# Sums of the Strassen blocks written back into PSUM, and the last down steps done in two halves of the columns: a transformer block on one core of Trainium2

## The chip, the cores and the metric

The kernel runs on one core of a Trainium2 chip. It has five engines that matter here: PE (TensorE, the matrix multiplier, with PEld for its weight loads), DVE (VectorE), ACT (ScalarE), POOL (GpSimd) and SP (SyncE, which here only issues DMAs). SBUF is the core's working memory, PSUM the small memory into which PE adds up its products, in banks of 128 partitions by 512 fp32 numbers. The metric is the device time in microseconds (us) of one execution. For the kernel before, the median of three is 1511.14 us (1509.85 to 1515.28).

## What is computed

One layer of a hybrid encoder on x of 1024 positions and width 1024, in fp32, cut to what matters here:

```python
h = rms_norm(x, norm1)
proj = h @ w_in                                   # q, k, v of two mixers, forget logits, gates
qa, ka, va, fa, qc, kc, vc, gates = jnp.split(proj, SPLITS, axis=-1)
o_a = forgetting_attention(qa, ka, va, log_sigmoid(fa + forget_bias))   # 8 heads x 64, causal
o_b = chunk_band_attention(qc, kc, vc, rel_bias)                        # 8 heads x 64, a band
g_a, g_b = jnp.split(jax.nn.sigmoid(gates), 2, axis=-1)
merged = g_a * (o_a @ w_branch_a) + g_b * (o_b @ w_branch_b)
x = x + merged @ w_out
x = x + jnp.square(jax.nn.relu(rms_norm(x, norm2) @ w_up)) @ w_down     # width 4096 inside
return rms_norm(x, final_norm)
```

## The kernel before

Everything is held transposed: features on the 128 partitions, positions along the free axis in two halves of 512 (`hs(h)`). An fp32 matrix is split into a high and a low part (`fp32r`), and a product is three matmuls: high by high, high by low, low by high. `split` (L277) does that for an activation, ACT the high part and, mostly, DVE the low one; `split_w` (L163) does it for a weight, ACT (or POOL) the high part (L165), POOL the low one (L167).

The large products are done by a Strassen-like scheme, in units. A unit (`strassen_steps`, from L522) forms a block of 256 output features by 1024 positions as four tiles of 128 x 512, from seven products (`PRODS`), of four steps of three matmuls each, in four PSUM banks. While the products run, the tiles are put together: ACT copies the first product, p1 (L553); DVE forms u2 = bank 1 + p1 (L555), c22 = bank 2 + u2 (L557) and c22 = bank 3 + c22 (L559), which is output tile (1,1); bank 0 is tile (0,0) as it stands; and cc = bank + u2 (L567) makes the two others. c22 and cc go to SBUF tiles, and the function `out` of the stage reads them there, bank 0 in PSUM. Units take turns at two sets of four banks.

The order of the work, with the times at which it stands in the profiled execution:

- 0 to 320 us: load and norm of x, then 8 units of q and k (`project_qk`; `out` multiplies by the norm, L577) in turn with 4 units of v (`project_v`, L595), whose tiles are transposed on PE into banks of the second set (`vtp`, L604), split by ACT (`vs`, L278) and DVE (L279), and stored to DRAM.
- 320 to 430 us: the gate units (`project_gate`; `gate_out`, L391: multiply by the norm, then a sigmoid on ACT, L392, and a store of z, L393), interleaved with the row maxima of the first two heads (`s`, L499 on PE, L506 on DVE), whose transposed result goes out on ACT's queue as `m_rows` (L514). For unit 7, the last, `GPOOL` puts three of the four multiplications on POOL.
- 444 to 740 us: attention of 16 heads, with the branch products as fillers. 740 to 820 us: the other branch products and the merge. 820 to 906 us: the output projection; its last blocks give the operands of the up product (`late_operands`; the high part of T4 is an ACT cast), and unit 28, the first of 16 up units, starts with them. Norm 2 is worked out inside that unit: `norm2_stat` before the fourth finished product, `norm2` at the end (`rms`, `newton`, `spread`).
- 906 to 1190 us: the up units (`out`: relu and norm in one DVE instruction, L929, square on ACT, L930, store, and differences for the down product, L937).
- 1190 to 1499.6 us: the down product, the same scheme turned round: the seven products A11, S1, S2, S3, S4, A12, A22 over 16 steps k each, four tiles m a step, with the activations read back from DRAM.
- 1499.6 us to the end, 1515.9 us: the finish of the left half (h = 0). The last three steps of A22 (k = 13 to 15) run tile by tile: 9 matmuls of 128 x 512 for each of four tiles m. As a tile ends, `between` adds the bank to the accumulator (L1025), ACT squares (L234), DVE adds up the squares (L235), and ACT scales by the final gain (L998). `finish` then works out the norm of all 512 positions (`n_s` on PE, L266, Newton steps on DVE, L240 to L244, spread over the partitions by PE, `n_b`, L250), copies it to SBUF (L1007), multiplies the eight tiles (DVE L1016 six of them, POOL L1014 two) and stores each as 128 x 512 (L1017).

A scheduler places the instructions of each engine; `TO`, `VO`, `AO` and `LO` mark those that keep the written order. `tc.issue_after` holds an instruction behind another one in that order only.

## Time and profile before

| | |
|---|---|
| median of three runs | 1511.14 us (1509.85 to 1515.28) |
| the profiled execution's own time | 1517.57 us |
| its span in the trace | 1515.9 us |
| PE busy | 1458.9 us, 96% of the span |
| DVE busy | 958.2 us, 63% |
| POOL busy | 871.5 us, 57% |
| ACT busy | 730.4 us, 48% |
| mean share of the granted clock of PE | 0.983 |
| read and written in DRAM | 179.42 and 86.34 MB |

In a row of the timeline stand the start, the busy time, the engine, the line, the operation with its tiles (out<-in, numbers left out), and the count of instructions that run on from one another; in brackets the idle time ahead of the instruction and what ended it. Rows of groups give busy time in all and the mean of one instruction in ns. The windows give busy time of each engine in a stretch of the span, the granted clock of PE, the DMA engines' share and GB/s. In a row of a DMA queue stand its packets, MB, and its share of the time of 16 DMA engines.

### The profile page before, as it was taken

What the parts mean: (1) busy time and instruction counts of PE and PEld (TensorE: products, weight loads), DVE (VectorE), ACT (ScalarE), POOL (GpSimd) and SP (SyncE); (2) the same over time, 40 slices, a digit from 0 to 9 for tenths busy, and PEclk for the clock granted to TensorE, in tenths of its full rate; (3) what the DMA queues carried; (4) which work ended last, traced back from release to release, by engine and by line L of the source; (5) the groups of instructions that cost most, each with busy time, mean ns of one, the idle gap of its engine ahead of it and who ended that gap; (6) DMA issues with size and microseconds to landing.
All of it is one profiled execution on the core that took longest, in us unless ns stands there. A gap on an engine that the chain in (4) does not pass through costs nothing.

```text
span 1515.9 us, 20994 instructions
## 1 busy us (share of the span) xinstructions
PE 1458.9 (96%) x6774; PEld 1208.0 (80%) x6774; DVE 958.2 (63%) x1528; ACT 730.4 (48%) x1388; POOL 871.5 (57%) x712
## 2 busy tenths in 40 slices
PE   8999999999889889999999999999999999999996
PEld 5777888888668778888787888888888888888885
DVE  7755456644368678766424687666666557999543
ACT  8633333254348768657524553333333344444643
POOL 2478787778742223111076467888888555558462
PEclk9999999999989989999999999999999999999998
DMA  8546678763587698876466424444443776589363
GB/s 268 153 117 171 186 196 227 184 203 128 166 186 182 157 169 198 191 197 162 155 198 209 165 73 167 153 152 151 151 151 132 248 261 200 154 253 222 93 205 115
DMA packets 153039, 267.18 MB, mean 176 GB/s; under 512 B 22552, under 2 KB 40216, under 8 KB 149792
## 3 DMA queue, kind: packets, MB, share of 16 engines
q1 hardware_dynamic: 78544, 141.02, 30.6%
q10 hardware_dynamic: 50448, 84.27, 17.6%
q0 software_dynamic: 23936, 40.54, 12.6%
q8 instruction: 53, 0.87, 0.2%
q14 instruction: 58, 0.48, 0.1%
HBM read 179.42 MB, written 86.34 MB: 175 GB/s over the span
## 4 chain that ended last, share of the span: by engine, by line
PE 41%; POOL 4%; DMA 2%; DVE 2%; issue 2%; ACT 1%; SPq 0%; DVEq 0%; ACTq 0%; POOLq 0%
PE u L218 19%; PE dS L218 9%; PE dA L218 8%; PE o L218 4%; POOL wl_S L167 1%; PE dA L96 1%; POOL m L835 1%; POOL ml L279 1%; DMA olt<-o_dram 1%; DMA wr<-wall 0%; POOL accw L991 0%; DMA rb<-r_dram 0%; DMA z<-z_dram 0%; DVE T2l L279 0%; DVE B22l L279 0%
## 5 line engine op out<-in xcount | busy, mean ns | idle before, releaser
L167 POOL TENSOR_TENSOR wl_A<-wr,wh_A 128x512 fp32r<-128x512 f32 x118 | 165.8, 1412 | 81.1 <-ACT wh_A L165 63.8
L167 POOL TENSOR_TENSOR wl_S<-S,wh_S 128x512 fp32r<-128x512 f32 x102 | 139.4, 1371 | 30.2 <-ACT wh_S L165 29.9
L279 DVE TENSOR_TENSOR tl<-p,th 128x512 fp32r<-128x512 f32 (+1 forms) x192 | 109.6, 593 | 30.6 <-ACT th L278 26.3
L165 ACT CAST wh_A<-wr 128x512 fp32r<-128x512 f32 x105 | 65.0, 620 | 102.2 <-DMA a_dram<-at 53.0
L165 ACT CAST wh_S<-S 128x512 fp32r<-128x512 f32 x105 | 63.8, 618 | 86.7 <-POOL S L190 35.5
L278 ACT CAST th<-p 128x512 fp32r<-128x512 f32 (+1 forms) x192 | 92.6, 509 | 12.2 <-PE pv L752 5.7
L167 POOL TENSOR_TENSOR wl_S<-ks,wh_S 128x512 fp32r<-128x512 f32 x48 | 68.1, 1446 | 52.6 <-ACT wh_S L96 48.7
L506 DVE CUSTOM_DVE_ANT_0 s<-s,bc 128x384 f32<-128x384 f32 (+3 forms) x128 | 69.8, 564 | 36.6 <-PE s L499 22.9
L499 PE MATMUL s<-qk 128*128 128x384 f32 (+2 forms) x192 | 63.4, 362 | 20.9 <-DMA qk<-qk_dram 14.5
L567 DVE TENSOR_TENSOR cc<-u,u 128x512 f32<-128x512 f32 x70 | 48.0, 686 | 54.9 <-PE u L218 54.7
L188 POOL TENSOR_TENSOR S<-wr,wr 128x512 f32<-128x512 f32 x35 | 49.5, 1415 | 56.8 <-DMA wr<-wall 51.0
L930 ACT ACTIVATE v<-v 128x512 f32<-128x512 f32 x64 | 40.5, 632 | 62.3 <-DVE v L929 62.3
L751 PE MATMUL pv<-th,v 128*128 128x512 f32 (+1 forms) x192 | 66.9, 348 | 1.0 <-ACT on L764 0.9
L728 PE MATMUL st<-qk 128*128 128x512 f32 (+1 forms) x192 | 67.0, 352 | 0.1
L736 PE MATMUL st<-sk 82*128 82x512 f32 (+1 forms) x192 | 66.1, 346 | 0.0
L752 PE MATMUL pv<-th,v 128*64 128x512 f32 (+1 forms) x192 | 66.0, 344 | 0.0
L753 PE MATMUL pv<-tl,v 128*128 128x512 f32 (+1 forms) x192 | 66.0, 344 | 0.0
L167 POOL TENSOR_TENSOR wl_A<-ka,wh_A 128x512 fp32r<-128x512 f32 x32 | 46.1, 1449 | 33.8 <-ACT wh_A L96 33.8
L278 ACT CAST qkh<-qk 128x512 fp32r<-128x512 f32 x32 | 19.9, 621 | 91.7 <-DMA qk_dram<-qkl 34.6
L748 ACT ACTIVATE p<-st,ncq 128x512 f32<-128x512 f32 (+1 forms) x96 | 54.0, 597 | 16.2 <-PE st L744 11.3
L499 PEld LDWEIGHTS s<-qk 128*128 128x128 f32 x192 | 36.7, 201 | 29.7 <-DMA qk<-qk_dram 13.5
L218 PE MATMUL u<-B11h,wh_A 128*128 128x512 f32 x140 | 56.2, 402 | 3.4 <-DVE vs L279 3.4
(404 smaller groups left out, 4959.6 us busy)
## 6 DMA issues: line engine op xcount, KB each, us to landing
wr<-wall SPq DMA_DIRECT2D x243, 256.0 KB
qk<-qk_dram POOLq DMA_DIRECT2D x16, 1024.0 KB, 6.3
a_dram<-at ACTq DMA_DIRECT2D x64, 256.0 KB
xT<-a_dram SPq DMA_DIRECT2D x64, 256.0 KB
qk_dram<-qkh ACTq DMA_DIRECT2D x96, 128.0 KB
a_dram<-v ACTq DMA_DIRECT2D x48, 256.0 KB
xB<-a_dram SPq DMA_DIRECT2D x44, 256.0 KB
z_dram<-zt ACTq DMA_DIRECT2D x32, 256.0 KB
```

What stands on the lines that cost most here:

```text
L165: (act.tensor_copy if act is G else act.copy)(wh, src)
L167: eng.tensor_tensor(wl, src, wh.bitcast(F32), op=ALU.subtract)
L218: done = eng.matmul(bank, w[wi], x[xi], start=(first and t == 0), stop=(t == n - 1 and not part), skip_group_check=part or not first)
L278: A.copy(dst[0], src)
L279: eng.tensor_tensor(dst[1], src, dst[0].bitcast(F32), op=ALU.subtract)
L499: T.matmul(ps[:, :n], qk[:, 1, i * P:(i + 1) * P], qk[:, 0, ks:ks + n], start=True, stop=not diag)
L506: V.tensor_tensor_reduce(ps[:, :v], ps[:, :v], bc[:, b0:b0 + v], 1.0, prev, ALU.add, ALU.min, out)
L728: T.matmul(ps[:, c], qk[:, 0, keys], qk[:, 1, qs], start=True, stop=False)
L736: T.matmul(ps[:, c], sk[:, 0, keys], sk[:, 1, qs], start=False, stop=not extra)
L751: T.matmul(pv[:, c], v3[hh][:, j, 1:3, :], th[:, c], start=first, stop=False)
L752: T.matmul(pv[0:HD, c], v3[hh][:, j, 0, :], th[:, c], start=False, stop=False)
L753: T.matmul(pv[:, c], v3[hh][:, j, 1:3, :], tl[:, c], start=False, stop=last)
```

## The change

**Sums stay in PSUM.** In every unit of projections, gates and up product, c22's last sum is written over bank 1, and the two cc over the banks that they are read from; `out` reads them in PSUM. No multiplication, sum, cast or store is dropped.

**Gates.** `GPOOL` becomes empty: the three multiplications of unit 7 go from POOL to DVE.

**The first up unit.** For k = 3 the high part of T4 is a DVE copy and not an ACT cast. The Newton steps of norm 2 and of the final norm keep v and t in columns 8 and 16 of the PSUM tile of the statistics. Unit 29's weight preparation is held behind unit 28's third-last low part (`behind`); POOL's order of those instructions is what it was.

**The end.** The last three steps of A22 run over two halves of 256 positions, q = 0 and 1, each with its own sums, squares and scaling; a half's norm is worked out by itself. For q = 0 the norm's sum stands behind q = 1's second tile on PE, the eight multiplications are on POOL and read a copy of the norm in SBUF, and its four stores (two tiles each, 128 x 2 x 256) are on SP. For q = 1 the eight multiplications are on DVE and read the norm in PSUM; its eight stores of 128 x 256 alternate between SP and ACT.

```diff
-GPOOL = (7,)
+GPOOL = ()
...
-    def rms(name, ps):
-        r = cpool.tile([P, 2, 4], F32, tag="nr", name=f"{name}_r", bufs=2)
-        v, y = r[:, 0, :], r[:, 1, :]
+    def rms(name, ps, n=4):
+
+        y, v, t = cpool.tile([P, 2, 4], F32, tag="nr", name=f"{name}_r", bufs=2)[:, 0, 0:n], ps[:, 8:8 + n], ps[:, 16:16 + n]
...
             elif n == 3:
-                V.tensor_tensor(c22, banks[3], c22, op=ALU.add)
-                out(1, 1, c22)
+                V.tensor_tensor(banks[1], banks[3], c22, op=ALU.add)
+                out(1, 1, banks[1])
...
-                t = mk("cc")
-                V.tensor_tensor(t, banks[b], u2, op=ALU.add)
-                out(*((0, 1) if n == 5 else (1, 0)), t)
+                V.tensor_tensor(banks[b], banks[b], u2, op=ALU.add)
+                out(*((0, 1) if n == 5 else (1, 0)), banks[b])
...
-        split(xop["T4", k], t2, V)
+        if k == 3:
+            V.tensor_copy(xop["T4", k][0], t2)
+            V.tensor_tensor(xop["T4", k][1], t2, xop["T4", k][0].bitcast(F32), op=ALU.subtract)
+        else:
+            split(xop["T4", k], t2, V)
...
-    def finish(ps_pool, h, tiles, engs):
-
-        y = norm_stat(ps_pool, f"n3_{h}", accs[h])
+    def finish(ps_pool, h, tiles, engs, q=0, w=HALF):
+
+        cols = slice(q * w, (q + 1) * w)
+        eng = T if h else TO
+        y = norm_stat(ps_pool, f"n3_{h}{q}", accs[h][:, cols], eng)
...
-                dst = t[:, m, :]
+                dst = t[:, m, cols]
                 if engs[n % len(engs)] is G:
-                    G.tensor_tensor(dst, dst, rstd[:, hs(h)], op=ALU.mult)
+                    G.tensor_tensor(dst, dst, scale, op=ALU.mult)
                 else:
                     V.tensor_tensor(dst, dst, pb, op=ALU.mult)
-                (load, store)[n % 2](outT[:, m + 4 * row, hs(h)], dst)
+                out = outT[:, :, h * HALF + q * w:h * HALF + (q + 1) * w]
+                if engs != (G,):
+                    (load, store)[n % 2](out[:, m + 4 * row, :], dst)
+                elif m % 2:
+                    load(out[:, m + 4 * row - 1:m + 4 * row + 1, :], t[:, m - 1:m + 1, cols])
...
-            rest = between(n, banks)
-            for m in range(4):
-                for k in range(15 - STAG, 16):
-                    multiply(m, k)
-                next(rest)
+            rest, w = iter(()), HALF // 2
+            for q in range(2):
+                cols = slice(q * w, (q + 1) * w)
+                for m in range(4):
+                    for k in range(15 - STAG, 16):
+                        multiply(m, k, cols)
+                    V.tensor_tensor(au[:, m, cols], banks[m][:, cols], au[:, m, cols], op=ALU.add)
+                    final(au, m, 1, 0, cols)
+                    if m % 2:
+                        next(rest, None)
+                for _ in rest:
+                    pass
+                rest = finish(psm[1], 0, (p1, au), (V,) if q else (G,), q, w)
```

How the change moves instructions is seen at three places. The first is PE's queue at the seam of unit 9 (q and k) and unit 17 (v); `vtp` are the transposes of the v tiles of unit 16, `u17_0` is unit 17's first bank. Before:

```order
L218 MATMUL u9_3_941<-T4h_122,wl_9_A22_936 128x512
L604 MATMUL vtp_1085<-ident_66,vt_848 128x128 x4
L604 MATMUL vtp_1098<-ident_66,vt_862 128x128 x4
L218 MATMUL u17_0_1214<-B11h_170,wh_17_A11_1180 128x512
L218 MATMUL u17_0_1214<-B11l_174,wh_17_A11_1180 128x512
L218 MATMUL u17_0_1214<-B11h_170,wl_17_A11_1182 128x512
L604 MATMUL vtp_1111<-ident_66,vt_878 128x128 x4
```

And with the change:

```order
L220 MATMUL u9_3_937<-T4h_122,wl_9_A22_932 128x512
L610 MATMUL vtp_1079<-ident_66,vt_846 128x128 x4
L610 MATMUL vtp_1092<-ident_66,vt_860 128x128 x4
L220 MATMUL u17_0_1208<-B11h_170,wh_17_A11_1174 128x512
L220 MATMUL u17_0_1208<-B11l_174,wh_17_A11_1174 128x512
L220 MATMUL u17_0_1208<-B11h_170,wl_17_A11_1176 128x512
L220 MATMUL u17_0_1208<-B11h_170,wh_17_A11_1174 128x512
L220 MATMUL u17_0_1208<-B11l_174,wh_17_A11_1174 128x512
L220 MATMUL u17_0_1208<-B11h_170,wl_17_A11_1176 128x512
L610 MATMUL vtp_1105<-ident_66,vt_875 128x128 x4
```

The third transpose stands one group of three matmuls later, and so does the fourth, further on; the same in the three other units of v.

The second place is the seam of the gates and attention, on POOL, before (`wl_ab` are low parts of branch weights, `sk0` rows of the first head's operands):

```order
L167 TENSOR_TENSOR wl_ab2_0_7164<-wr21_0_7160,wh_ab2_0_7162 128x512
L391 TENSOR_TENSOR zt_4034<-c22_3750,rstd_96 128x512
L167 TENSOR_TENSOR wl_ab3_0_7435<-wr21_3_7431,wh_ab3_0_7433 128x512
L167 TENSOR_TENSOR wl_ab4_0_7608<-wr22_0_7604,wh_ab4_0_7606 128x512
L391 TENSOR_TENSOR zt_4108<-cc_4106,rstd_96 128x512
L391 TENSOR_TENSOR zt_4144<-cc_4142,rstd_96 128x512
L167 TENSOR_TENSOR wl_ab5_0_7862<-wr22_3_7858,wh_ab5_0_7860 128x512
L703 DMA sk0_4214<-m_rows_101 2x1024
```

With the change the last two of them stand on DVE, between the row maxima (`s`) of head 0:

```order
L573 TENSOR_TENSOR u7_2_3712<-u7_2_3712,u2_3715 128x512
L395 TENSOR_TENSOR zt_4071<-u7_2_3712,rstd_96 128x512
L510 ISA s_4017,st_4016<-s_4017,bc0_0_2889 128x384
L510 ISA st_4016 128x1
L573 TENSOR_TENSOR u7_3_3713<-u7_3_3713,u2_3715 128x512
L510 ISA s_4020,mn0_0_3897<-s_4020,bc0_0_2889,st_4016 128x256
L510 ISA mn0_0_3897 128x1
L395 TENSOR_TENSOR zt_4106<-u7_3_3713,rstd_96 128x512
```

The unit's last sums are the same instructions as before with another target; the three `zt` are new on this queue, the last of them behind head 0's last maximum (`mn0_0`), and POOL's low parts have nothing between them now.

The third place is the end of the program. PE before, from the last product of the last tile (`n3_0_s` the sums of squares, `n3_0_b` the spread norm):

```order
L96 MATMUL dA22_3_14911<-xT4h15_15206,wh_A22_15_15210 128x512
L96 MATMUL dA22_3_14911<-xT4l15_15207,wh_A22_15_15210 128x512
L96 MATMUL dA22_3_14911<-xT4h15_15206,wl_A22_15_15212 128x512
L266 MATMUL n3_0_s_15282<-ones_71,rstd_96 128x1 x4
L250 MATMUL n3_0_b_15296<-ident_66,n3_0_r_15287 128x128 x4
```

With the change, at the end of the second half's second tile (`n3_00` is the norm of the first half, `n3_01` that of the second):

```order
L96 MATMUL dA22_1_14836<-xT4l15_15134,wh_A22_15_15137 128x256
L96 MATMUL dA22_1_14836<-xT4h15_15133,wl_A22_15_15139 128x256
L96 MATMUL n3_00_s_15237<-ones_71,rstd_96 128x1 x2
L96 MATMUL dA22_2_14837<-xT4h13_15087,wh_A22_13_15093 128x256
L96 MATMUL dA22_2_14837<-xT4l13_15088,wh_A22_13_15093 128x256
```

And behind the last tile's products:

```order
L96 MATMUL dA22_3_14838<-xT4l15_15134,wh_A22_15_15137 128x256
L96 MATMUL dA22_3_14838<-xT4h15_15133,wl_A22_15_15139 128x256
L96 MATMUL n3_00_b_15276<-ident_66,n3_00_r_15240 128x128 x2
L96 MATMUL n3_01_s_15292<-ones_71,rstd_96 128x1 x2
L96 MATMUL n3_01_b_15303<-ident_66,n3_01_r_15295 128x128 x2
```

The first half's sum is in the stream of products now, its spread directly behind the last product. And on DVE, with the change, from the last tile's sum on:

```order
L1116 TENSOR_TENSOR accu_12289<-dA22_3_14838,accu_12289 128x256
L246 TENSOR_SCALAR n3_00_s_15237<-n3_00_s_15237 128x2
L237 TENSOR_TENSOR rstd_96<-rstd_96,sq_15258 128x256
L247 TENSOR_TENSOR n3_00_r_15240<-n3_00_r_15240,n3_00_s_15237 128x2
L237 TENSOR_TENSOR rstd_96<-rstd_96,sq_15272 128x256
L276 TENSOR_SCALAR n3_01_s_15292<-n3_01_s_15292 128x2
L243 RECIPROCAL n3_01_r_15295<-n3_01_r_15295 128x2
L244 TENSOR_TENSOR n3_01_s_15292<-n3_01_s_15292,n3_01_r_15295 128x2
L245 TENSOR_TENSOR n3_01_s_15292<-n3_01_s_15292,n3_01_r_15295 128x2
L246 TENSOR_SCALAR n3_01_s_15292<-n3_01_s_15292 128x2
L247 TENSOR_TENSOR n3_01_r_15295<-n3_01_r_15295,n3_01_s_15292 128x2
L1034 TENSOR_TENSOR accp1_12288<-accp1_12288,n3_01_b_15303 128x256 x4
```

The first half's last Newton steps stand behind the last tile's sum, two instructions apart, and the eight multiplications of the second half (four of them are the last row) follow its own Newton steps.

More of the change, by code (lines that the diff above doesn't have):

```diff
@@ L248, in spread @@
         pb = ps_pool.tile([P, HALF], F32, tag="d", name=f"{name}_b")
-        for c in range(4):
+        for c in range(y.shape[1]):
             eng.matmul(pb[:, c * P:(c + 1) * P], y[:, c:c + 1].to_broadcast([P, P]), ident, start=True, stop=True)
@@ L520, in strassen_unit, with strassen_steps @@
             pass
-    def strassen_steps(u, ps_pool, mk, out, start=(), between=None, before=None, cut=0):
-        ws = strassen_w(u, V if between else G, ALL[:cut] if cut else FIRST if between else ALL)
+    def strassen_steps(u, ps_pool, mk, out, start=(), between=None, before=None, cut=0, behind=()):
+        with ExitStack() as order:
+            for ins in behind:
+                order.enter_context(tc.issue_after(ins))
+            ws = strassen_w(u, V if between else G, ALL[:cut] if cut else FIRST if between else ALL)
         late, out_ = [], out
@@ L938, in out @@
                 store(a_dram[XI[n], u], t)
-        strassen_unit(U_UP + u, psm[u % 2], etile3, out, start=() if u else START2, before=None if u else (norm2_stat, norm2))
+        strassen_unit(U_UP + u, psm[u % 2], etile3, out, start=() if u else START2, before=None if u else (norm2_stat, norm2),
+                      behind=late)
+        late = () if u else (lows[-3].ins,)
     hstack.close()
@@ L1005, in finish @@
             yield
-        pb = spread(ps_pool, f"n3_{h}", y)
-        A.copy(rstd[:, hs(h)], pb)
+        pb = spread(ps_pool, f"n3_{h}{q}", y, eng)[:, 0:w]
+        scale = accs[h][:, cols]
+        if G in engs:
+            A.copy(scale, pb)
         yield
```

43 lines of the change are left out of this document (22 added, 21 removed).

## The prediction

> **What bounds the kernel now.** I read the engines' shares first, then the windows by stage, to see where PE stands still; then the waits and the timeline at those places, and the groups of instructions for the prices. The page's row of engines:
>
> ```profile
> PE 1458.9 (96%) x6774; PEld 1208.0 (80%) x6774; DVE 958.2 (63%) x1528; ACT 730.4 (48%) x1388; POOL 871.5 (57%) x712
> ```
>
> PE bounds the whole; DVE is busy 63% of the time. The windows give start and end, length, busy time of PE, PEld, DVE, ACT and POOL, the granted clock, the DMA share and GB/s:
>
> ```profile
> 120.00:136.00 16.00, 12.60 (x49) 10.01 (x48) 8.28 (x16) 6.91 (x16) 12.59 (x10) 0.89 0.77 224
> 400.00:444.00 44.00, 32.13 (x136) 25.02 (x134) 22.88 (x64) 11.25 (x20) 30.32 (x30) 0.87 1.01 246
> 444.00:740.00 296.00, 283.19 (x1585) 244.84 (x1585) 212.90 (x584) 218.84 (x478) 64.74 (x93) 0.96 0.72 170
> 906.00:1366.00 460.00, 460.00 (x2031) 380.50 (x2030) 324.12 (x335) 184.79 (x314) 323.31 (x239) 1.00 0.55 181
> 1499.60:1515.90 16.30, 3.06 (x16) 2.68 (x16) 6.06 (x15) 2.27 (x5) 2.49 (x2) 0.65 0.35 129
> ```
>
> In up and most of down (906 to 1366) PE is busy for 460.00 of 460.00 us at the full clock, so no other engine's work can be bought off there. PE stands still in four places: 3.4 us near 128, 11.9 us before attention, 12.8 us inside it, and 13.2 of the last 16.3 us. A change of DVE's work can pay only there.
>
> **The sums in PSUM.** Their prices, from the groups of instructions (busy us in all, mean ns of one):
>
> ```profile
> L929 DVE SCALAR_TENSOR_TENSOR v<-cc,rstd 128x512 f32<-128x512 f32 x32 | 51.8, 1619 | 0.5
> L929 DVE SCALAR_TENSOR_TENSOR v<-u,rstd 128x512 f32<-128x512 f32 x16 | 11.0, 690 | 18.2 <-PE u L218 17.8 <-ACT rstd L921 0.4
> L567 DVE TENSOR_TENSOR cc<-u,u 128x512 f32<-128x512 f32 x70 | 48.0, 686 | 54.9 <-PE u L218 54.7
> L506 DVE CUSTOM_DVE_ANT_0 s<-s,bc 128x512 f32<-128x512 f32 x40 | 28.2, 704 | 3.0 <-PE s L499 2.2 <-PE s L502 0.6
> ```
>
> The consumer that reads cc in SBUF takes 1619 ns, the one that reads bank 0 in PSUM 690: some 0.9 us less for each of 32 tiles, 29.7 us of DVE in the up stage alone, if the PSUM reader's price holds. The sum itself costs 686 ns; written over PSUM I take it at 704, the price of the row maxima that write over their own bank. All of it lies beside a PE that is busy for every microsecond of 906 to 1366, so it brings nothing there. The place where it could is a wait for DVE:
>
> ```profile
> 119.35 1.52 DVE L595 TENSOR_TENSOR vt<-c,rstd 128x512 f32<-128x512 f32 x1
> 127.30 0.65 ACT L278 CAST vs<-vtp 128x256 fp32r<-128x256 f32 x2 [4.01 <-DMA wr<-wall]
> 127.70 0.76 DVE L279 TENSOR_TENSOR vs<-vtp,vs 128x256 fp32r<-128x256 f32 x2 [2.57 <-ACT vs L278]
> 128.18 0.50 PE L218 MATMUL u<-B11h,wh_A 128*128 128x512 f32 x1 [3.40 <-DVE vs L279]
> PE u L218 <- DVE vs L279: 3.4, 1, 3.4
> PE u L218 <- DVE c L557: 0.7, 1, 0.7
> ```
>
> PE waits for DVE's split of a transpose bank, but DVE waited 2.57 us for ACT there, and ACT 4.01 us for a DMA. The faster vt at 119.35 is 7 us too early to matter. I take 0 for the sums. Below: the 0.7 us wait for c goes. Above: the moved transposes are three matmuls later in four units, 12 x 0.227 = 2.7 us (the pitch is in the next rows but one), if the banks that they free are waited for in each; before, PE waits for them in one unit only. What hides the 0 is slack of the bank sets, which alternate from unit to unit.
>
> **The gates.** Three multiplications go from POOL to DVE, and the z stores behind them are earlier in ACT's queue:
>
> ```profile
> L391 POOL TENSOR_TENSOR zt<-cc,rstd 128x512 f32<-128x512 f32 x2 | 2.5, 1274 | 0.4 <-DVE cc L567 0.4
> 438.13 0.33 ACTq L393 DMA_DIRECT2D z_dram<-zt  x1
> 438.83 2.18 PE L499 MATMUL s<-qk 128*128 128x256 f32 x7 [2.74 <-DMA qk<-qk_dram]
> 445.30 0.63 PE L736 MATMUL st<-sk 82*128 82x512 f32 x1
> ```
>
> On DVE two of them stand ahead of row maxima of head 0, 2 x 0.7 = 1.4 us; PE then waits 2.74 us for the second head's qk by DMA, which covers them; without this cover they cost 1.4. On ACT the stores of z now stand ahead of head 0's `m_rows`. I take 0. Below: one POOL multiplication, 1.3 us, off the way of the branch weights' low parts. Above: two z stores of 256 KB ahead of the qk load: 512 KB at the window's 246 GB/s is 2.1 us.
>
> **Attention** is reshuffled by the scheduler with the same instructions. Of 12.8 us of idle PE I allow a quarter, 3.2 us, either way, and take 0.
>
> **The first up unit.** Two rows of the timeline:
>
> ```profile
> 894.06 0.62 ACT L278 CAST T4h<-t 128x512 fp32r<-128x512 f32 x1 [5.19 <-DVE t L866]
> 895.73 0.50 PE L218 MATMUL u<-B21h,wh_A 128*128 128x512 f32 x1 [0.20 <-ACT p L553]
> ```
>
> Without the T4h cast ACT copies p 0.62 us earlier, and PE's wait of 0.20 us goes: -0.2. T4l isn't earlier, since DVE makes the copy itself, about as long. `behind` moves nothing in POOL's order: 0. The Newton scratch in PSUM changes no length that the end of the unit waits for by more than 0.1: 0.
>
> **The end.** The timeline from the last product on:
>
> ```profile
> 1499.17 0.39 PE L96 MATMUL dA<-xT4h,wl_A 128*128 128x512 f32 x1
> 1499.60 0.69 DVE L1025 TENSOR_TENSOR accu<-dA,accu 128x512 f32<-128x512 f32 x1
> 1500.32 0.63 ACT L234 ACTIVATE sq<-accu 128x512 f32<-128x512 f32 x1 [0.65 <-DVE accu L1025]
> 1501.73 1.05 PE L266 MATMUL n_s<-ones,rstd 128*128 128x1 f32 x8 [2.17 <-DVE rstd L235]
> 1502.82 0.16 DVE L272 TENSOR_SCALAR n_r<-n_s 128x4 f32<-128x4 f32 x1 [1.14 <-PE n_s L266]
> 1504.34 2.01 PE L250 MATMUL n_b<-ident,n_r 128*128 128x128 f32 x8 [1.56 <-DVE n_r L244]
> 1506.39 0.59 ACT L1007 COPY rstd<-n_b 128x512 f32<-128x512 f32 x1 [3.11 <-PE n_b L250]
> 1507.01 1.88 DVE L1016 TENSOR_TENSOR accp<-accp,n_b 128x512 f32<-128x512 f32 x3 [2.72 <-ACT rstd L1007]
> 1507.72 0.96 SPq L1017 DMA_DIRECT2D outT<-accp  x2
> ```
>
> Three phases follow on one another: norm (1499.6 to 1506.4), multiplications, stores. The half-width prices come from tiles of 256 columns elsewhere: two matmuls in attention, then DVE's and ACT's split of the v transposes, and POOL's low part of `near` (shortest, median, longest ns):
>
> ```profile
> 459.93 0.28 PE L751 MATMUL pv<-th,v 128*128 128x256 f32 x1
> 460.04 0.28 PE L752 MATMUL pv<-th,v 128*64 128x256 f32 x1
> 1498.94 0.39 PE L96 MATMUL dA<-xT4l,wh_A 128*128 128x512 f32 x1
> L278 ACT CAST vs<-vtp x32: 365/374/384, 120.8 to 253.2; 128x256 fp32r<-128x256 f32 x32
> L279 DVE TENSOR_TENSOR vs<-vtp,vs x32: 406/416/426, 121.2 to 253.6; 128x256 fp32r<-128x256 f32 x32
> L279 POOL TENSOR_TENSOR nbl<-near,nbh x8: 717/735/746, 332.7 to 530.5; 128x256 fp32r<-128x256 f32 x8
> ```
>
> And the stores, as the DMA view has them for 1506 to 1516 (40 slices of 0.25 us, then one of the two hardware queues), with the software queue of 510.5 to 515, whose packets are of 512 bytes:
>
> ```profile
> GB/s 0 0 0 0 0 0 0 0 0 0 287 369 344 402 385 393 360 385 393 393 377 377 377 360 402 369 369 385 385 385 401 393 99 0 0 0 0 0 0 0
> q1 hardware_dynamic: 576, 1.05, 28.6%
> q0 software_dynamic: 496, 0.25, 29.1%
> ```
>
> Data flows from 1508.5, 0.8 after the first store is issued, at about 375 GB/s until 1514.1; the span ends 1.8 later. Let T be 1499.6, when the last product is done; before, the span ends at T+16.3.
>
> PE: 72 matmuls at 0.118 (half the pitch of 1498.94 to 1499.17, and near the 0.11 of 459.93 to 460.04) for 36 at 0.227 are 8.50 for 8.17, +0.3; the first half's `n_s` in line, half of 1.05, +0.5: the last product is done at T+0.8. From there, in us:
> - the last sum 0.42, a Newton step 0.2, the third tile's squares 0.4, the last Newton step 0.2: the first norm at 1.2;
> - its spread on PE, half of 2.01, to 2.2; the copy (0.37) to 2.65; POOL from 2.7, a pair every 2 x 0.735: 4.2, 5.6, 7.1, 8.6;
> - the second half's `n_s` to 2.75, its Newton steps as before (1502.82 to 1504.34, 1.5) to 4.3, its spread to 5.3; DVE's eight multiplications at 0.42 from 5.4 to 8.8;
> - stores: the first pair's data from 5.0 (0.8 after its end), 0.26 MB, done by 5.9; the second pair's from 6.4, and from there both engines give more than the DMA takes, so 1.83 MB flow at its rate.
>
> That rate is the open price: a row of a store is 1 KB now and was 2 KB. A packet of 0.5 KB took 0.291 x 4.5 us x 16 / 496 = 42 ns of an engine, one of the tail (1.82 KB on average) 0.286 x 10 us x 16 / 576 = 79 ns. The line between them gives 56 ns for 1 KB, 16 x 1.024 KB / 56 ns = 290 GB/s. So 1.83 MB take 6.3 us, until 12.7; with 1.8 behind, T+0.8+14.5 = T+15.3, and the end gains 1.0. At 375 GB/s it would be 4.9 us, a gain of 2.4; at 195, the rate of the 0.5 KB packets (16 x 0.512 KB / 42 ns), 9.4 us, a loss of 2.1. I take 290, which the two rows give.
>
> The Trainium skill ("DMA: Bandwidth & Descriptors", Specifications) says that a transfer of 512 bytes or more runs at line rate; by it the rows of 1 KB would lose nothing, and the end would gain 2.4. The 42 ns of a 0.5 KB packet, which are half the time of one over three times its size, speak against it, though that queue is POOL's.
>
> **The sum**: -1.0 - 0.2 = -1.2. The profiled execution took 1517.57 us, 1.67 over its span; it would take 1516.4. It was 6.4 over the median of the runs, and the same difference from that, 1511.14 - 1.2, is 1509.9, the forecast.
>
> **Rivals.**
> *The stall at 128 goes (faster).* The PSUM sums shift DVE's and ACT's work in the v units, and the split comes before it is waited for. It would give the 3.40 us of idle and the lowered clock around it, 16 us x (1 - 0.89) = 1.8: 5.2 in all, 1504.7. For it: the chain's last link is DVE, which loses 0.8 us a tile in these units. Against it: DVE waited there itself, and the transposes now come later. 0.13.
> By the Trainium skill ("TensorE: Matmul & The Clock Gate", Part 1) the clock halves after an idle window of about 3.4 us that is free-running; the trace agrees in the size of this one wait, followed by a clock of 0.89 in that window.
> *Attention is entered later (slower).* The z stores ahead of the second head's qk load delay it by 2.1 us, and PE's 2.74 of waiting becomes 4.8. It decides from the point where it is longer than the 3.40 us after which the clock was lowered at 128: then another 1.8 is lost at that clock. -1.2 + 2.1 + 1.8 = +2.7: 1513.8. For it: the DMA share is 1.01 there. Against it: a matmul at 445.30 takes 0.63 instead of 0.39, so that the clock is lowered there already, and part of it can't be lost again. 0.15.
> *The stores of 1 KB run as fast as those of 2 KB.* The end gains 2.4: 1511.14 - 2.6 = 1508.5. For it: DVE and POOL give enough, and a hardware queue may do better than the software one. Against it: the line of packets above. 0.12.
> *The scheduler's new order in attention is worth more than 3.2 us*, in either direction: 1506 or 1514 at least. Nothing in the profile tells which. 0.06.
> The forecast keeps 0.54.
>
> **Range and chances.** The forecast's own range: the bounds of the parts, put together as independent ones: down 1.4 (end), 0.7, 1.3, 3.2, in all 3.8; up 3.1, 2.7, 2.1, 3.2, in all 5.6: 1506.1 to 1515.5. To hold 8 in 10 it reaches down through the first rival with half of that spread, to 1503.0, and up to 1515.5, which takes in the second rival. A measurement of this kernel can tell about 0.5%, 7.6 us, from no change: faster is below 1503.6, slower above 1518.7. Below lie two fifths of the first rival (0.05), half of the scheduler's case on that side and the forecast's tail: 0.12. Above, little of the second rival and the other tail: 0.04. The rest, 0.84, is the same.
>
> **What would show it.** Right: cc's consumers at about 0.7 us and DVE's busy time some 30 us lower in up alone, with PE's 906 to 1366 unchanged; the last product 0.8 later against the stage's start; the norm of the first half used on POOL while the second is worked out; stores at about 290 GB/s; a span after T of some 15.3. Wrong: the stall near 128 gone, or a new one with the transposes; more than 11.9 us of idle PE between 400 and 444; stores at 375 GB/s or at 195; or a wait of PE inside the last 72 matmuls for the first half's squares.

## The result and the profile after

The changed kernel takes 1506.1 us in the median of 12 runs (1499.28 to 1510.48), the kernel before 1512.39 in 12 (1506.77 to 1518.69). The ratio is 0.9947, with a 95% interval from 0.9931 to 0.9962: 8.0 us less by the ratio, between 5.7 and 10.4 (the two medians alone are 6.3 apart), where 1.2 less was forecast. The two profiled executions are 12.0 us apart (1517.57 and 1505.53), because that of before lies at the upper end of its runs; so a difference between these two traces counts here only where other traces show it too.

The row of engines of the changed kernel, and its window over up and most of down:

```profile
PE 1452.9 (97%) x6810; PEld 1205.7 (80%) x6810; DVE 890.9 (59%) x1548; ACT 733.1 (49%) x1396; POOL 841.6 (56%) x715
906.00:1366.00 460.00, 460.00 (x2031) 380.59 (x2029) 283.11 (x340) 186.32 (x315) 311.25 (x245) 1.00 0.57 180
```

DVE has 67 us less to do and up is still PE's alone. What was not expected is POOL: 29.9 us less, of which the three multiplications that left it explain 3.8. A part of that, 9.6 us, lies in one of its groups. First the low parts of weights as before had them, then with the change, then the consumer of up and the sum over the bank with the change:

```profile
L167 POOL TENSOR_TENSOR wl_A<-wr,wh_A 128x512 fp32r<-128x512 f32 x118 | 165.8, 1412 | 81.1 <-ACT wh_A L165 63.8 <-ACT wh_A L96 15.6 <-DMA outT<-accw 1.7
```

```profile
L169 POOL TENSOR_TENSOR wl_A<-wr,wh_A 128x512 fp32r<-128x512 f32 x118 | 156.2, 1332 | 88.0 <-ACT wh_A L167 69.3 <-ACT wh_A L96 11.7 <-PE dA L96 3.3
L940 DVE SCALAR_TENSOR_TENSOR v<-u,rstd 128x512 f32<-128x512 f32 x64 | 43.9, 688 | 20.1 <-PE u L220 18.1 <-ACT rstd L931 1.0
L573 DVE TENSOR_TENSOR u<-u,u 128x512 f32<-128x512 f32 x70 | 48.8, 697 | 66.8 <-PE u L220 66.8
```

The same 118 instructions of POOL take 80 ns less each, though nothing in them was changed. One of the gate units shows it instruction by instruction. Timeline of before, DVE and POOL:

```profile
357.74 1.29 POOL L190 TENSOR_TENSOR S<-S,wr 128x512 f32<-128x512 f32 x1
357.75 1.83 DVE L391 TENSOR_TENSOR zt<-c,rstd 128x512 f32<-128x512 f32 x1
358.99 1.76 POOL L205 TENSOR_TENSOR wr<-wr,wr 128x512 f32<-128x512 f32 x1
360.70 1.29 POOL L167 TENSOR_TENSOR wl_A<-wr,wh_A 128x512 fp32r<-128x512 f32 x1
363.19 0.69 DVE L391 TENSOR_TENSOR zt<-cc,rstd 128x512 f32<-128x512 f32 x1
363.33 1.70 POOL L208 TENSOR_TENSOR S<-wr,S 128x512 f32<-128x512 f32 x1
```

The same place with the change:

```profile
351.05 1.30 POOL L192 TENSOR_TENSOR S<-S,wr 128x512 f32<-128x512 f32 x1
352.30 1.31 POOL L207 TENSOR_TENSOR wr<-wr,wr 128x512 f32<-128x512 f32 x1
352.95 0.69 DVE L395 TENSOR_TENSOR zt<-u,rstd 128x512 f32<-128x512 f32 x1
```

Before, DVE's multiplication reads c22 and the norm in SBUF; it starts 0.01 us behind POOL's sum, takes 1.83 instead of 0.69, and the next instruction of POOL takes 1.76 instead of 1.31. With c22 in PSUM both have their shorter length, though DVE's multiplication runs beside POOL's sum there too. So this tile cost DVE over 1 us and POOL 0.45. Who pays depends on who starts first: in the last two rows of before DVE starts 0.14 us ahead and has its 0.69, and POOL's sum takes 1.70.

POOL's queue also issues the loads of qk for the heads. Issue and use of the first of them, before:

```profile
399.77 0.74 POOL L483 DMA_DIRECT2D qk<-qk_dram  x1
412.56 0.58 PE L499 MATMUL s<-qk 128*128 128x256 f32 x1 [5.70 <-DMA qk<-qk_dram]
406.00:420.00 14.00, 8.30 (x32) 6.48 (x31) 5.27 (x10) 4.95 (x9) 9.10 (x9) 0.88 0.68 220
```

And with the change (the third row of each is the window around the wait):

```profile
390.98 0.75 POOL L487 DMA_DIRECT2D qk<-qk_dram  x1
403.31 0.36 PE L503 MATMUL s<-qk 128*128 128x256 f32 x1 [1.26 <-DMA qk<-qk_dram]
401.00:415.00 14.00, 12.74 (x58) 10.31 (x57) 8.98 (x22) 4.91 (x8) 10.78 (x14) 1.00 0.85 225
```

PE came to this matmul at 412.56 - 5.70 = 406.86 and comes at 402.05 now, 4.8 us earlier; POOL issues the load 8.8 us earlier. The load has gained 4.0 us on PE, and the wait has shrunk by 4.4. With the granted clock, 0.88 and now 1.00 over 14 us, that place is worth 4.4 + 1.7 = 6.1 us between these two traces. The load stands at the same place in POOL's order in both kernels; POOL only comes to it sooner. Its last 70 instructions ahead of the load are the same in both. The window that they fill, before and then with the change:

```profile
284.84:399.77 114.93, 114.27 (x505) 94.29 (x504) 50.13 (x60) 47.03 (x82) 88.10 (x70) 1.00 0.51 154
```

```profile
280.26:390.95 110.69, 110.69 (x490) 91.70 (x489) 40.33 (x59) 47.22 (x82) 83.37 (x70) 1.00 0.53 158
```

POOL is busy for 4.7 us less with the same work, about what the load has gained on PE.

### The profile page after: what moved, and what is told of

Same layout as the page of the kernel before. It is cut to its first block, busy times and chain, and to the rows that moved or that the text cites. A ratio compares the mean times of both kernels' runs of the same rounds, so it can differ in the third digit from the quotient of the medians.

```text
span 1503.8 us, 21101 instructions
## 1 busy us (share of the span) xinstructions
PE 1452.9 (97%) x6810; PEld 1205.7 (80%) x6810; DVE 890.9 (59%) x1548; ACT 733.1 (49%) x1396; POOL 841.6 (56%) x715
## 4 chain that ended last, share of the span: by engine, by line
PE 77%; DMA 9%; DVE 6%; issue 3%; POOL 2%; ACT 2%; ACTq 1%; SPq 0%; POOLq 0%; DVEq 0%
PE u L220 40%; PE dS L220 12%; PE dA L220 8%; PE o L220 4%; DMA qk<-qk_dram 4%; PE m L220 3%; DMA rb<-r_dram 2%; PE pv L757 1%; PE pv L758 1%; PE pv L759 1%; PE s L503 1%; PE st L734 1%; PE st L742 1%; DVE s L510 1%; PE st L750 1%
## 5 line engine op out<-in xcount | busy, mean ns | idle before, releaser
L169 POOL TENSOR_TENSOR wl_A<-wr,wh_A 128x512 fp32r<-128x512 f32 x118 | 156.2, 1332 | 88.0 <-ACT wh_A L167 69.3
L573 DVE TENSOR_TENSOR u<-u,u 128x512 f32<-128x512 f32 x70 | 48.8, 697 | 66.8 <-PE u L220 66.8
L190 POOL TENSOR_TENSOR S<-wr,wr 128x512 f32<-128x512 f32 x35 | 45.5, 1301 | 66.3 <-DMA wr<-wall 66.1
L754 ACT ACTIVATE p<-st,ncq 128x512 f32<-128x512 f32 (+1 forms) x96 | 54.9, 597 | 22.8 <-PE st L750 17.3
L220 PE MATMUL u<-B22h,wh_S 128*128 128x512 f32 x140 | 54.8, 392 | 2.5 <-DVE c L564 2.5
```

Source lines behind the costliest of these rows:

```text
L169: lows.append(eng.tensor_tensor(wl, src, wh.bitcast(F32), op=ALU.subtract))
L220: done = eng.matmul(bank, w[wi], x[xi], start=(first and t == 0), stop=(t == n - 1 and not part), skip_group_check=part or not first)
```

## Experiments

The theory after the result (theory 1 below): a DVE instruction with two operands in SBUF and a POOL instruction stand in each other's way; the sums in PSUM leave DVE one operand in SBUF; POOL becomes shorter, what it issues and prepares comes sooner, and waits of PE behind that shrink. The rival (theory 2): the sums are hidden as predicted, and the gain is order and the timing of DMAs. All ratios are to the kernel before.

**The sums and the gates alone.** Only the sums in PSUM and `GPOOL = ()`:

```diff
-GPOOL = (7,)
+GPOOL = ()
...
-                V.tensor_tensor(c22, banks[3], c22, op=ALU.add)
-                out(1, 1, c22)
+                V.tensor_tensor(banks[1], banks[3], c22, op=ALU.add)
+                out(1, 1, banks[1])
...
-                t = mk("cc")
-                V.tensor_tensor(t, banks[b], u2, op=ALU.add)
-                out(*((0, 1) if n == 5 else (1, 0)), t)
+                V.tensor_tensor(banks[b], banks[b], u2, op=ALU.add)
+                out(*((0, 1) if n == 5 else (1, 0)), banks[b])
```

Expected: 

> The kernel before with the sums in PSUM and unit 7's multiplications on DVE, nothing else of the change. Theory 1 (the sums carry the gain: DVE reads one operand in PSUM, no longer stands in POOL's way in SBUF, both get shorter, and the waits near 128 and 412 us shrink with the half-clock windows behind them): 6 to 9 us faster than before; cc's consumers at 0.7 us, POOL's low parts some 3 to 6% shorter, PE's wait near 128 us under 1 us. Theory 2 (the prediction: the sums are hidden, the gain of the whole change is a different order and the DMAs' timing): within 2 us of before, with the 3.4 us wait near 128 still there.

Measured: 1504.37 us, ratio 0.996 (0.9942 to 0.9979), 6.0 us faster. The low parts `wl_A` take 1330 ns, the wait near 128 us is 0.67, that for head 0's qk is gone (under 0.3). This part of the change carries most of its gain.

**The end alone**, in the kernel before: `final`, `finish` and the last steps as in the diff of the change, with the Newton scratch in SBUF:

```diff
-            yield from finish(psm[1], 0, (p1, au), (V, V, G))
...
+                rest = finish(psm[1], 0, (p1, au), (V,) if q else (G,), q, w)
```

Expected: 

> The kernel before with only the end in two halves of the columns; Newton scratch in SBUF as before. The prediction: 1.0 us faster, from the first tail product to the end 23.7 us where before has 24.7. Rival, from the trace of the whole change: products half as wide need the operands of k = 14 and 15 about 0.9 us sooner than POOL gives them, PE waits 1.5 us and the clock halves for one window: from the first tail product to the end 26 us, 1.4 us slower than before.

Measured: 1510.27 us, ratio 0.9998 (0.9979 to 1.0017). From the first tail product to the end of the span it took 23.8 us where the traced execution of before took 24.6. That is between the two expectations and nearer the first; the time can't tell 1 us.

**The changed kernel with the old end.**

```diff
-                rest = finish(psm[1], 0, (p1, au), (V,) if q else (G,), q, w)
...
+            yield from finish(psm[1], 0, (p1, au), (V, V, G))
```

Expected: 

> The changed kernel with the old end (full-width last steps, one finish for the left half). If the new end costs 1.4 us, this is 1 to 2 us faster than the changed kernel, 8 to 10 us faster than before; if it gains the predicted 1.0, this is 1 us slower than the changed kernel, 5 to 7 us faster than before.

Measured: 1502.75 us, ratio 0.9946 (0.9924 to 0.9967). Its interval holds both what the first and what the second case says; against the changed kernel's 0.9947 no difference is seen.

**Step k first in the first half of the end.**

```diff
+                if q == 0:
+                    for k in range(15 - STAG, 16):
+                        for m in range(4):
+                            multiply(m, k, cols)
                 for m in range(4):
-                    for k in range(15 - STAG, 16):
+                    for k in range(15 - STAG, 16) if q else ():
                         multiply(m, k, cols)
```

Expected: 

> The changed kernel with the first half's last products ordered by step k first and tile m second (the second half by tile as it is). If the end loses by operands that come late, the two waits for POOL's low parts in the tail (0.75 and 0.74 us) and the half-clock window behind them go, and from the first tail product to the end it takes 23 to 24 us where the changed kernel took 26.1: 2 to 3 us faster than the changed kernel. If the halved clock has another cause (short products as such), PE still runs at a pitch of 0.21 in the tail and the time is that of the changed kernel within 1 us.

Measured: 1501.62 us, ratio 0.9937 (0.9917 to 0.9957). The two waits are gone and from the first tail product to the end it takes 22.8 us. But so it does without this edit in three later traces of the changed end (22.1 to 22.9), so that these waits are not in each execution; in time the run is not told apart from the changed kernel.

**The sums in PSUM in the units of q, k and v alone**, and then **in the gate units alone** (the latter with `GPOOL = ()`):

```diff
+IN_PSUM = lambda u: 8 <= u < 20
...
-                V.tensor_tensor(c22, banks[3], c22, op=ALU.add)
-                out(1, 1, c22)
+                t = banks[1] if IN_PSUM(u) else c22
+                V.tensor_tensor(t, banks[3], c22, op=ALU.add)
+                out(1, 1, t)
...
-                t = mk("cc")
+                t = banks[b] if IN_PSUM(u) else mk("cc")
```

In the second kernel the condition is `u < 8`.

Expected of the first: 

> The kernel before with the sums in PSUM in the units of q, k and v alone. Theory 1, as the traces so far have it (POOL is slowed while DVE reads two SBUF operands, its weight loads are issued later, and what waits for them stands still): the 3.2 to 3.4 us wait near 128 us goes, with its half-clock window, 4 to 5 us; the 5.4 to 5.7 us wait for head 0's qk near 412 stays by 3 us or more, since POOL is still slowed in the gate units. 4 to 6 us faster than before. Rival (the wait near 128 is a matter of chance in the DMAs): it is there again, and the time within 2 us of before.

Expected of the second: 

> The kernel before with the sums in PSUM in the gate units alone and unit 7's multiplications on DVE. Theory 1: the wait near 128 us stays at 3.2 to 3.4 us; POOL gains some 0.45 us for each tile of the gate units that DVE read in SBUF, some 3 us by 400 us, so that the wait for head 0's qk near 412 is 3 us or less, and one half-clock window less: 2 to 4 us faster than before. Rival (the order of the whole program, not the port): the wait near 412 stays above 5 us, the time within 2 us of before.

Measured: 1511.26 us, ratio 0.9991 (0.9967 to 1.0016), for the first, and 1505.03 us, ratio 0.9973 (0.9939 to 1.0006), for the second. Waits for head 0's qk, the projections alone:

```profile
408.20 0.58 PE L500 MATMUL s<-qk 128*128 128x256 f32 x1 [5.90 <-DMA qk<-qk_dram]
```

and the gates alone:

```profile
405.06 0.36 PE L500 MATMUL s<-qk 128*128 128x256 f32 x1 [1.29 <-DMA qk<-qk_dram]
```

That wait is settled by the sums of the gate units, as theory 1 said. The times settle nothing: both intervals hold 1, and in the first the 4 to 6 us are not seen. The two gains, 0.0009 and 0.0027 of the time, add up to 0.0036, near the 0.0040 of both together. And the wait near 128 us was 0.65 us in the first, as expected, but 0.99 in the second, whose program is that of before up to the gate units. Here theory 1 missed.

**Three useless sums in every unit of the changed kernel**, once with both operands in SBUF, once with one of them in PSUM. Nothing reads their results:

```diff
                 V.tensor_tensor(banks[1], banks[3], c22, op=ALU.add)
                 out(1, 1, banks[1])
+                V.tensor_tensor(p1, u2, p1, op=ALU.add)
...
                 V.tensor_tensor(banks[b], banks[b], u2, op=ALU.add)
                 out(*((0, 1) if n == 5 else (1, 0)), banks[b])
+                V.tensor_tensor(p1, u2, p1, op=ALU.add)
```

In the second kernel `banks[1]` and `banks[b]` stand for `u2` in the added lines.

Expected with both in SBUF: 

> The changed kernel, and in every Strassen unit three more DVE sums of two SBUF tiles of 128 x 512 in SBUF that nobody uses. If it is the two SBUF operands of a DVE instruction that slow POOL, the three take 0.7 us alone and some 1.1 to 1.7 beside POOL, POOL's low parts go back from 1.33 to some 1.4 us, and the waits near 128 and 412 us come back by 2 us or more each: 5 to 8 us slower than the changed kernel, about the time of before. If the gain comes from DVE's freed time or the order, this one and the next run alike.

Expected with one in PSUM: 

> The same three useless sums in every unit, but with one operand in PSUM. If it is the two SBUF operands, they take 0.7 us each, POOL's low parts stay at 1.33 us, the waits near 128 and 412 stay under 1.3 us, and the time is that of the changed kernel within 2 us. If DVE's time itself was what counted, it is as much slower as the run with two SBUF operands.

Measured: with both in SBUF 1516.58 us, ratio 1.0044 (1.003 to 1.0059); with one in PSUM 1499.85 us, ratio 0.9938 (0.9911 to 0.9964). The groups with both in SBUF:

```profile
L169 POOL TENSOR_TENSOR wl_A<-wr,wh_A 128x512 fp32r<-128x512 f32 x118 | 175.9, 1499 | 71.5 <-ACT wh_A L167 54.6 <-ACT wh_A L96 14.4 <-PE dA L220 1.9
L576 DVE TENSOR_TENSOR p<-u,p 128x512 f32<-128x512 f32 x70 | 107.2, 1532 | 2.0
```

With one in PSUM:

```profile
L169 POOL TENSOR_TENSOR wl_A<-wr,wh_A 128x512 fp32r<-128x512 f32 x118 | 158.1, 1349 | 96.9 <-ACT wh_A L167 81.4 <-ACT wh_A L96 11.6 <-PE dA L96 2.1
L576 DVE TENSOR_TENSOR p<-u,p 128x512 f32<-128x512 f32 x70 | 47.6, 679 | 0.1
```

The rows are those of 70 of the 105 sums; the 35 behind c22 take 1095 and 680 ns. The same number of sums of the same size, and the kernels are 1.06% apart, 16 us. With one operand in PSUM they take DVE 71 us, and nothing of it is seen in the time. With both in SBUF they take 146 us, and POOL's low parts 1499 ns instead of 1349. So two operands in SBUF are what costs, for both engines. By which of the two the 16 us come was not as expected: PE did not wait for qk near 412 but three times for DVE's c22, 5.1 us in all, the longest 2.7, and twice for ACT's p, 2.7 us. Here the longer sums held up DVE's own queue ahead of c22 (two of them took 3.36 us just ahead of the longest of these waits), so this pair shows the price of the operands, and not the way by POOL and the load.

**The kernel before twice more, and the changed kernel without the sums.**

```diff
-                V.tensor_tensor(banks[1], banks[3], c22, op=ALU.add)
-                out(1, 1, banks[1])
+                V.tensor_tensor(c22, banks[3], c22, op=ALU.add)
+                out(1, 1, c22)
...
-                V.tensor_tensor(banks[b], banks[b], u2, op=ALU.add)
-                out(*((0, 1) if n == 5 else (1, 0)), banks[b])
+                t = mk("cc")
+                V.tensor_tensor(t, banks[b], u2, op=ALU.add)
+                out(*((0, 1) if n == 5 else (1, 0)), t)
```

Expected of the second profile: 

> The kernel before once more, for a second profile. If the wait for head 0's qk near 412 us belongs to this code, it is there with more than 4 us. The wait near 128 us was 3.4 and 3.2 us in two profiles of code with its sums in SBUF there, and 0.99 in a third: if it belongs to the code it is over 3 us here, if it is a matter of chance it may be anything between 0.5 and 3.5.

Expected of the third: 

> The kernel before a third time, for another profile: the wait for head 0's qk near 412 us again over 4 us if it belongs to the code; the wait near 128 us over 3 us if it does, anything between 0.5 and 3.5 if it is a matter of chance.

Expected without the sums: 

> The changed kernel with the sums in SBUF as before: what is left is unit 7's multiplications on DVE, the first up unit, and the end. Theory 1 (the sums carry the gain): the wait for head 0's qk is over 3 us, cc's consumers take 1.1 to 1.6 us, and the time is that of before within 2.5 us. Rival (the three multiplications taken off POOL, or the rest, carry it): 4 us or more faster than before, the wait under 2 us.

Measured: 1512.7 and 1519.3 us in one run each; without the sums 1512.63 us, ratio 1.0012 (0.999 to 1.0035). The second profile of before:

```profile
127.67 0.52 PE L218 MATMUL u<-B11h,wh_A 128*128 128x512 f32 x1 [3.08 <-DVE vs L279]
411.03 0.58 PE L499 MATMUL s<-qk 128*128 128x256 f32 x1 [5.65 <-DMA qk<-qk_dram]
```

The changed kernel without the sums:

```profile
407.91 0.58 PE L503 MATMUL s<-qk 128*128 128x256 f32 x1 [5.16 <-DMA qk<-qk_dram]
PE u L220 <- DVE vs L283: 1.0, 1, 1.0
```

The traces together, with the waits of PE in us:

| kernel | sums in PSUM | near 128 | head 0's qk |
|---|---|---|---|
| before, three executions | none | 3.40, 3.08, 2.88 | 5.70, 5.65, 5.24 |
| before with the new end | none | 3.23 | 5.39 |
| changed, without the sums | none | 1.02 | 5.16 |
| projections alone | q, k, v | 0.65 | 5.90 |
| gates alone | gates | 0.99 | 1.29 |
| sums and gates | all | 0.67 | under 0.3 |
| changed, old end | all | 1.20 | 0.71 |
| changed | all | 0.63 | 1.26 |
| changed, step k first | all | 0.68 | under 0.3 |
| changed, useless sums with one operand in PSUM | all | 1.41 | 1.21 |
| step k first, q and k read in PSUM (below) | all | under 0.3 | under 0.3 |
| changed, useless sums with both operands in SBUF | all | under 0.3 | under 0.3 |

The last column follows the sums of the gate units: 5.2 to 5.9 us in six traces without them, 1.3 or less in the others. POOL's 70 instructions ahead of the load go with it: 87.8 to 89.5 us busy in those six, 82.7 to 83.9 in the seven with the sums ahead of the last row. That row stands apart: there POOL needs 88.8 us as without the sums, but PE comes to head 0 only at 414.0, later than with the sums in any other trace, so that the load is in time all the same. Without the sums nothing of the gain is left.

The wait near 128 is not settled: it is 1.4 or less wherever q, k and v have their sums in PSUM, but it was about 1.0 in two executions that had not, and in the third of before it was under the 3 us expected. And it matters about as much as the other. Leaving the last row out, head 0's first matmul starts at 411.0 to 416.5 us in the four traces in which both waits are long, at 407.9 and 408.2 in the two in which only that for qk is, and at 400.1 to 405.1 in the seven in which both are short. From there to the first tail product it takes 1071 to 1080 us in all fourteen traces, with the sums and without them. So the gain lies ahead of that matmul, and in these traces roughly half of it comes at the wait near 128, of which it isn't shown that the sums removed it.

**One more subtraction with an operand in PSUM.** With step k first, and the scaled tile of q and k written over its bank, so that the split reads it there:

```diff
-            t = etile("qk")
+            t = src
             V.scalar_tensor_tensor(t, src, -0.125 if row == 0 else 1.0, rstd[:, hs(h)], op0=ALU.mult, op1=ALU.mult)
```

Expected: 

> The changed kernel with the first half's last products by step k first, and in the q and k units the scaled tile written over its PSUM bank too, so that the split's subtraction reads one operand in PSUM and one in SBUF. Theory 1: those 32 subtractions take 0.7 us instead of up to 1.65, PE's wait of 1.4 us near 119 us (for DVE behind such a subtraction) goes, POOL is slowed in fewer places: 0 to 3 us faster than the run with step k first, 1496 to 1501 us in the median. If PE hides all of it, the same as that run within 1.5 us.

Measured: 1502.76 us, ratio 0.9943 (0.9921 to 0.9966). The 32 subtractions take 687 ns (with the change 681 to 1811), and no wait over 0.3 us stands between 98 and 419 us; but the time is no better than that of the run with step k first (0.9937). PE's waits there were short already, and what is saved is less than these runs resolve.

## Why the prediction was wrong in size

The sign and the range hold (1506.1 lies between 1503.0 and 1515.5), and by the prediction's own bound of 1503.6 us the time counts as the same, which had 0.84 of the chance; by the ratio it is 0.53% less (0.38 to 0.69), at the edge of that. But the forecast of 1.2 us is a seventh of what came (a fifth by the medians), and the mechanism was another one. That the range holds 1506.1 with room is owed to its reach down for the first rival, whose reason isn't shown: in part luck. (1504.7 less half of 3.8 would be 1502.8 and not 1503.0, which decides nothing.)

**The sums.** The failed step is "The place where it could is a wait for DVE", and with it the term "I take 0 for the sums": only waits that DVE itself ends were looked at. In its place the runs show a wait for a load that POOL issues, 5.2 to 5.9 us without the sums of the gate units and 1.3 or less with them; the rest of the gain, at the wait near 128, stays open. The prices were right: 688 ns for up's consumers where 690 was taken, 697 and 699 for the sums over a bank where 704 was; up gained nothing. But the 1619 ns of a consumer in SBUF were read as DVE's own length and not as a sign that it stood in POOL's way. POOL's 1.76 beside 1.29 stood in the same trace, and POOL's queue with the qk load behind it was not followed. The prediction did put both places of the gain, 128 and the 11.9 idle us before attention, among those where DVE's work could pay, and then looked in the second only at the multiplications that move. (Its four places hold 41.3 of PE's 57.0 idle us; most of the others lie ahead of 120 us and in the merge.)

The Trainium skill ("SBUF — State Buffer", Who interferes with whom, and its Summary) says that a DVE instruction with two inputs in SBUF contends with a GpSimd instruction that reads SBUF, and that the one that comes second is blocked until the other is done. The traces agree to about 0.14 us: the DVE instruction that started 0.01 us behind POOL's 1.29 took 1.83, which is the rest of that and 0.55, where its own length is 0.69; POOL's next, which started 0.59 us ahead of that one's end, took 1.76, for 0.59 and its own 1.31.

**The gates.** The forecast of 0 for the three multiplications on DVE holds: with them and without the sums the ratio is 1.0012. The rival that attention is entered later did not come: the load of head 0's qk came sooner. The wait of 2.74 us that the prediction gives to the second head's qk is one for the third head's, by the order of POOL's loads (issued at 425.31, the third; the second, at 404.74, had landed before PE asked). With the change it is 3.78 us. The load takes longer, 15.6 us from issue to landing for 13.5, and PE comes 1.0 us later behind its issue. It is not the z stores: with them moved and without the sums the load takes 12.4 us and the wait is 2.31. In the six traces without the sums of the gate units the load takes 11.6 to 13.6 us, in the eight with them 14.6 to 15.6; what slows it is open.

**The stall at 128** did go, as the first rival said, in the changed kernel, and the 6.4 us that this rival takes off 1511.14 are, of the first three rivals, nearest to what came. Its reason, that DVE's chain is shorter, isn't shown, since the stall was also short twice without it. A trace of before shows what ends it: ACT waits for the landing of a weight load.

**Attention.** From about 440 to 740 us of before, and the same stretch with the change:

```profile
440.00:740.00 300.00, 285.86 (x1596) 246.60 (x1596) 215.53 (x595) 219.10 (x479) 65.29 (x94) 0.96 0.71 170
```

```profile
431.00:729.50 298.50, 283.48 (x1595) 244.10 (x1594) 212.24 (x595) 219.84 (x479) 64.82 (x94) 0.97 0.70 169
```

PE stands still for 14.1 us and for 15.0, and the stretch is 1.5 us shorter: within the 3.2 allowed either way, so that the fourth rival's 1506, near as it is, did not come about by its reason.

**The first up unit.** PE's 0.20 us wait for p went, but a wait for DVE's c22 came. Timeline with the change:

```profile
881.52 1.39 DVE L875 CAST T4h<-t 128x512 fp32r<-128x512 f32 x1
882.95 1.66 DVE L876 TENSOR_TENSOR T4l<-t,T4h 128x512 fp32r<-128x512 f32 x1
885.99 0.50 PE L220 MATMUL u<-B22h,wh_S 128*128 128x512 f32 x1 [1.11 <-DVE c L564]
```

"T4l isn't earlier, since DVE makes the copy itself, about as long" was mis-sized: the copy takes 1.39 us where ACT took 0.62, and T4l 1.66 where it took 0.69, both beside POOL, and c22 is late behind them. (The copy reads one tile in SBUF and not two; no run shows its length without POOL beside it.) So -0.2 became +0.9 in this trace and in two others with the new first unit; in the four others the new wait isn't there.

**The end.** Forecast: the last product 0.8 us later, the rest 14.5 behind it. In the changed kernel's trace:

```profile
1477.71 0.28 PE L96 MATMUL dA<-xT4h,wh_A 128*128 128x256 f32 x1
1479.21 0.39 PE L96 MATMUL dA<-xT4h,wl_A 128*128 128x256 f32 x1 [0.75 <-POOL wl_A L169]
1480.88 0.38 PE L96 MATMUL dA<-xT4h,wl_A 128*128 128x256 f32 x1 [0.74 <-POOL wl_A L169]
1482.00 0.41 PE L96 MATMUL dA<-xT4h,wh_A 128*128 128x256 f32 x1
1490.81 0.42 DVE L1116 TENSOR_TENSOR accu<-dA,accu 128x256 f32<-128x256 f32 x1 [0.38 <-PE dA L96]
1474.00:1488.00 14.00, 12.47 (x73) 11.20 (x71) 5.59 (x11) 6.31 (x13) 3.52 (x3) 0.88 0.03 10
```

PE waited 1.5 us for low parts that the shorter products ask for sooner, and the clock was lowered (0.88 over 14 us, a pitch of 0.21). The products took 13.1 us instead of 8.4, 4.7 more and not 0.8. In this one execution the end lost 1.5 us against before (26.1 from the first tail product to the end, for 24.6). In the four other traces with the same end the products take 1.0 to 1.8 us more than in this trace of before, and from the first of them to the end of the span it is 22.1 to 23.8 us, for 24.6 to 27.3 in the seven traces with the old end. So the traces put the gain nearer to 2 us (the medians are 22.9 and 25.1) than to the 1.0 forecast; the times can't tell either from nothing. The term was mis-sized in both parts: PE took a little longer than forecast as a rule, and what follows it less, 12.8 to 13.7 us for 14.5. The stores of the changed kernel, 1490 to 1504 in slices of 0.35 us, and one of its queues:

```profile
GB/s 0 0 0 0 0 0 0 0 0 0 0 0 0 0 0 281 351 117 3 316 339 360 290 357 334 331 351 337 348 331 342 345 342 348 182 12 0 0 0 0
q1 hardware_dynamic: 1664, 1.57, 34.2%
```

They run at about 340 GB/s, not at 290 and not at 375: a packet took 0.342 x 14 us x 16 / 1664 = 46 ns, where the line drawn through the software queue's packets gave 56. The Trainium skill's rule ("DMA: Bandwidth & Descriptors", Specifications) of line rate from 512 bytes on isn't borne out to the full: rows of 1 KB ran a tenth slower than the 375 of rows of 2 KB.

## What to carry to other kernels

An engine's instruction that takes twice as long in one group as in another with the same shape may be held up by something else: look at what the other engine does in the same microseconds, and then at what stands behind that engine in its queue, loads included. Here a tile that stayed in PSUM cost DVE nothing and gave POOL its time back, and about half of the gain came out at a load that POOL issued sooner; the other half lies at the wait near 128 us, and its cause is open. Work taken off an engine can be worth it even where PE hides that work, if the engine's operands stand in another's way.

## What the runs showed of the hardware that was not expected

- A DVE sum of 128 x 512 takes 679 ns in the mean with one operand in PSUM and one in SBUF, and 1532 with both in SBUF in a kernel whose POOL is busy 58% of the time; POOL's low parts of that shape go from 1349 to 1499 ns with it.
- At this size a DVE instruction with an operand in PSUM is as fast as one with both in SBUF to some 10 ns: 688 ns in the mean for up's consumers in PSUM, 674 to 681 for the shortest of the consumers in SBUF.
- Stores in rows of 1 KB ran at about 340 GB/s, in rows of 2 KB at about 375.
